# A two-layer decoder step on one core: the first norm's squares and product, the score pairs and the final norm are placed anew

## The chip, the cores and the metric

The kernel runs on one core of one Trainium2 chip. TensorE (PE) multiplies, VectorE (DVE), ScalarE (ACT) and GpSimd (POOL) work on tiles in SBUF, SyncE (SP) mostly issues DMA transfers, as ACT can too. The metric is the device time of one execution in microseconds; three runs of the kernel before gave 601.29 us as median, from 601.08 to 602.26.

## The reference, cut to what matters

One step of a decoder with two layers for 264 tokens: a prompt of 256 and eight samples of one token each, 1024 features wide. All weights are shared.

```
def rmsnorm(x, g):
    y = xf * lax.rsqrt(jnp.mean(xf * xf, axis=-1, keepdims=True) + EPS)
    return (y * g).astype(x.dtype)
...
def moba_gmlp_mixer(...):          # layer 0
    h = rmsnorm(x, norm_g)
    z = h @ w_in                   # q, k, v, bu, bv of 512 each
    q, k = rope_partial(q), rope_partial(k)
    a = moba_attention(q, k_all, v_all, pos)
    bvn = layer_norm(jax.nn.gelu(bv), sgu_gain)
    b_out = spatial_gating(jax.nn.gelu(bu), bvn, sgu_w, sgu_b)
    return x + jnp.concatenate([a, b_out], -1) @ w_out, new_kv, bvn
...
def conv_ffn(...):
    h = rmsnorm(x, norm_g)
    a = jax.nn.gelu(causal_conv(h @ w_gate)) * (h @ w_up)
    return x + a @ w_down, ...
```

Layer 1 has stick-breaking attention and a pooling mixer in place of the two mixers of layer 0; a final rmsnorm gives y. The outputs are y, the new keys and values of both layers, and some small states.

## The kernel before, in words

Activations lie transposed: 128 features on the partitions, the 264 tokens (T) along the free axis, so the 1024 features are eight tiles (KD) of 128 x 264. Every weight matrix is cut into blocks of 128 x 128, and all blocks of the whole step stand in memory in the order in which TensorE uses them: 1472 blocks, one stream. Eight blocks make a tile of the stream. A chunk of one tile (chunks 0 to 5) or two (from chunk 6 on) comes by one DMA (`raw`, line 279). To keep fp32 accuracy each tile is split into a high part wh (an ACT copy, line 299, or line 631 for the first tiles) and a rest wl (a DVE subtraction, line 300 or 632); four buffers each, so a split runs up to three tiles ahead (`LOOK`). Each operand is split alike (xg_h, xg_l; `operand_tile`, line 384). A block is three matmuls: wh by xh, wh by xl, wl by xh. `run` (line 305) walks the order of a phase, asks for splits, issues the three matmuls, calls `evac` when an output tile is complete, and calls hooks that are due at a certain block; `blk(b, f)` (line 863) puts f behind block b of the phase.

The phases are, for each layer: in (160 or 128 blocks), out, ff (gate and up), dn (down). The change touches the first phase, in0, and what comes after the last.

The start: six packed pieces (`xw`) bring the first two tiles of weights and x; ACT, DVE and POOL work in an order that the source fixes with `keep_in_program_order` (lines 634 to 650); everything else is ordered by the planner of the tile framework, which runs its own model of the times. In in0 the first four output tiles, bv, are computed before the first norm's scale is known. The squares of x (ACT, `Norm.add`, line 397) are summed by POOL (lines 408 and 411); the last square stays alone, so the sum over partitions is made by two matmuls with a tile of ones into one PSUM bank (`rstd_of`, line 424; one matmul in fp32 is two rows in the trace). Ln and Exp on ACT (lines 431, 432) turn it into R. This is `norm0` (line 654), a hook behind block 30; it also scales the rope tables by R and then evacuates the bv tiles that were held. From block 32 on q, from 64 on k, from 96 on bu, from 128 on v are computed; their evacuations (lines 687 to 695) use R. `s_qk(t)` (line 707) multiplies q and k of a pair of heads: first a mask matmul (line 710), then the scores S (lines 712, 714); `s_tr` transposes their softmax. `gm_mean` and `gm_var` (lines 814, 817) are the layer norm of the gating branch: the sum over four tiles (bsum, lines 802 to 804), a product with ones (pmu), and the squares. SP issues nearly all DMAs in the order of the source; `page_regs` (line 338) loads page numbers into registers on the same queue, each of them three small instructions.

The end: the last phase evacuates each of its eight output tiles into X (line 598), squares it, lets POOL add the square, and multiplies X by the final gain (line 603). After the last tile come its add, its square, two products with ones (ns_fin), Ln and Exp, five multiplications by R over 1, 2, 2, 2 and 1 feature tiles (line 1109, `YD`), and after each the DMA of its part of y from SP or ACT (line 1110).

Of the kernel before, what the change touches and what calls it, by code (L numbers as in the profile page):

```python
# [18 lines left out]
P = 128  # L19
# [3 lines left out]
NS = 8  # L23
# [12 lines left out]
MMB = 4  # L36
KQ = 5
WARM = 12
YD = ((0, 1), (1, 3), (3, 5), (5, 7), (7, 8))

NEG = -1e30
SCALE = HD ** -0.5
# [108 lines left out]
def _consts():  # L151
# [41 lines left out]
    ("sguw", (P, 512)), ("sgub", (P, 512)), ("poolw", (P, 512)),  # L193
]
_OUTS = [
    ("y", (KD, P, T)), ("k0", (P, 4, T)), ("v0", (P, 4, T)), ("bvn", (P, 4, NS)),
    ("k1", (P, 4, T)), ("v1", (P, 4, T)), ("poolp", (P, 4, NST)), ("pools", (P, 4, NS, 16)),
    ("cv0", (P, NF, 10)), ("cv1", (P, NF, 10)), ("cs0", (P, NF, NS)), ("cs1", (P, NF, NS)),
]
# [3 lines left out]
def tile_decoder_step(ctx: ExitStack, tc: tile.TileContext, a):  # L203
# [30 lines left out]
    def mv(name):  # L234
        return [f4(f"{name}_{x}", dt=F32R) for x in "hl"]
# [37 lines left out]
    def late(dst, src):  # L273
        tc.keep_in_program_order(nc.sync.dma_start(dst, src))
# [14 lines left out]
    pos = [0]  # L289

    def split(t):
        for tt in range(len(splits), min(t + (2 if t == 3 else LOOK), NT - 1) + 1):
            ci = chunk_of[tt]
            for c in range(ci, min(ci + 3, len(_CHUNKS))):
                raw(c)
            o = (tt * 8 - coff[ci]) * P
            src = raws[ci][:, o:o + 8 * P]
            h, l = splits[tt] = wtiles(tt)
            s.activation(h, src, AF.Copy)  # L299
            v.tensor_tensor(l, src, h.bitcast(F32), ALU.subtract)  # L300
        return splits[t]

    spare = (32, 40)
# [34 lines left out]
    def page_regs(n):  # L338
        for i in range(len(regs), len(regs) + n):
            regs.append(nc.sync.value_load(PT[0:1, i:i + 1], min_val=0, max_val=NPHYS - 1))  # L340
# [16 lines left out]
        page_regs(2)  # L357
    late(CS, a["rope"].rearrange("p (c t) -> p c t", c=2))
    raw(5)
    page_regs(4)  # L360
    late(CST, a["cst"])
    raw(6)
    page_regs(4)
    late(VEC, a["vec"])
    page_regs(4)
    GAIN = first[0][0]
    xin = [x[:, i, :] for _, _, x in first for i in range(x.shape[1])]
    tc.keep_in_program_order(s.preload_act_table_set("natural_log_exp_and_others"))
# [21 lines left out]
            tc.keep_in_program_order(j)  # L390

    class Norm:
        def __init__(self, name, two=False):
            self.name, self.two, self.last = name, two, []
            self.acc = None

        def add(self, m, src=None):
            q = sm.tile([P, T], F32, tag="sq", name=f"sq_{self.name}{m}")
            i = s.activation(q, X[:, m, :] if src is None else src, AF.Square)
            if src is not None:  # L400
                tc.keep_in_program_order(i)
            if m == KD - 1 and self.two:
                self.last.append(q)
            elif self.acc is None:
                self.acc = q
            elif m == 1:
                n = sm.tile([P, T], F32, tag="acc", name=f"acc_{self.name}", bufs=2)
                g.tensor_tensor(n, self.acc, q, ALU.add)
                self.acc = n
            else:  # L410
                g.tensor_tensor(self.acc, self.acc, q, ALU.add)

        def finish(self, pin=False):
            return rstd_of([self.acc] + self.last, 1.0 / D, self.name, pin)
# [6 lines left out]
        def finish2(self):  # L421
            return rstd_of(self.hl, 1.0 / D, self.name, w=onesr)

    def rstd_of(parts, scale, name, pin=False, bank=None, w=None):
        p = (bank or at)(f"ns_{name}")
        for i, x in enumerate(parts):
            mm = pe.matmul(p[:, :T], ones if w is None else w, x, start=i == 0, stop=i == len(parts) - 1)
            if pin:
                tc.keep_in_program_order(mm)
        R = sm.tile([P, T], F32, tag="R", name=f"R_{name}", bufs=2)  # L430
        s.activation(R, p[:, :T], AF.Ln, bias=epst, scale=scale)
        last[0] = s.activation(R, R, AF.Exp, scale=-0.5)
        return R

# [114 lines left out]
    def ffn(l, xg, nrm, down_evac, hooks=None):  # L549
# [7 lines left out]

        def norm():
            nonlocal R
            R = nrm.finish2()  # L560
            gelu_set()


# [25 lines left out]
        lnexp()  # L589
        run(orders[f"dn{l}"], lambda m, k: hl(act, k), down_evac, hooks)  # L590

    def residual(gain, name, operand=True):
        xg = [mv(f"xg_{name}{i}") for i in range(2)] if operand else None
        nrm = Norm(name, not operand)

        def evac(m, o):
            m = m[1]
            v.tensor_tensor(X[:, m, :], X[:, m, :], o, ALU.add)
            if operand:
                operand_tile(xg[m // 4], m, X[:, m, :], gain[:, m:m + 1])  # L600
            nrm.add(m)
            if not operand:
                s.activation(X[:, m, :], X[:, m, :], AF.Copy, scale=gain[:, m:m + 1])
        return xg, nrm, evac

    def pick(xg):
        return lambda m, k: hl(xg, k)
# [3 lines left out]


    xg = [mv(f"xg_0{i}") for i in range(2)]
    nrm = Norm("n0", True)
    for tt in range(2):
        splits[tt] = wtiles(tt)

# [19 lines left out]
    for m in range(1, 5):  # L637
        part(m, s)()
        operand_tile(xg[m // 4], m, xin[m], GAIN[:, m:m + 1], pin=True)
        if m != 2:  # L640
            nrm.add((m - 1) // 2 if m < 4 else 2, xin[(m - 1) // 2 if m < 4 else 2])
    whole(2)
    for m in range(5, KD):
        operand_tile(xg[m // 4], m, xin[m], GAIN[:, m:m + 1], pin=True)
    for m in range(3, KD):
        nrm.add(m, xin[m])
        if m == 4:
            whole(3)
        elif m == 6:
            whole(4)  # L650
    rope = f4("rope")
    R0, held = [], []
# [291 lines left out]
    st1 = {}  # L944

    qz1 = sample_z("l1")

    def norm1():
        nonlocal R
        R = nrm1.finish2()  # L950
        sigmoid_set()

    edge = f4("edge", (P, 384))
# [150 lines left out]
    _, nrm, evac = residual(vec("fin"), "fin", operand=False)  # L1104
    ffn(1, xg, norm_f, evac)
    R = nrm.finish()
    for i, (m, e) in enumerate(YD):
        x = X[:, m:e, :]
        v.tensor_tensor(x, x, R.unsqueeze(1).to_broadcast([P, e - m, T]), ALU.mult)  # L1109
        (s if i % 2 else nc.sync).dma_start(a["y"][m:e].rearrange("m p t -> p m t"), x)  # L1110


def _lay(inp):
# [66 lines left out]
```

## Time and profile before

| what | value |
|---|---|
| median of three runs | 601.29 us (601.08 to 602.26) |
| the profiled execution, its own time | 602.49 us |
| its span, first to last instruction | 600.7 us |
| mean granted TensorE clock | 0.995 |
| DVE, ACT, POOL busy in the span | 422.9, 343.3, 107.9 us |
| DMA | 122.42 MB, mean 204 GB/s |

A row of the timeline gives start, duration (both us), engine, line, operation, what it writes and reads with the shape, and how often it is repeated in the row; in square brackets stand the idle time of the engine ahead of it and what ended it. PE is TensorE's matmuls, PEld its weight loads; a "q" behind an engine is its queue. In a row of stretches come the stretch, its length, the busy time and number of instructions for each engine shown, the granted clock, the busy share of the DMA engines, and GB/s. Matmuls overlap in the pipeline, so that a PE row's duration is longer than its slot.

### The profile page before, as it was taken

The numbers are of one execution on the slowest core, as the hardware profiler recorded it, in microseconds if no ns is written. First come the engines' busy times: TensorE is split into PE (matmuls) and PEld (weight loads), VectorE is DVE, ScalarE is ACT, GpSimd is POOL, SyncE is SP. The second block draws the span as 40 slices with busy tenths as digits, with TensorE's granted clock in tenths as the row PEclk, the third lists the DMA queues.
The fourth block names the chain that finished last, engine by engine and source line by source line (L and its number), as shares of the span: only waits on it lengthen the run. The fifth ranks groups of instructions, "written<-read, shape, count | busy, mean of one in ns | idle before, by whom it ended". The sixth has DMA issues, their size and how long they took to land.

```text
span 600.7 us, 12394 instructions
## 1 busy us (share of the span) xinstructions
PE 588.6 (98%) x4900; PEld 569.6 (95%) x4900; DVE 422.9 (70%) x733; ACT 343.3 (57%) x600; POOL 107.9 (18%) x103
## 2 busy tenths in 40 slices
PE   8999999999999999999999999999999999999994
PEld 6988879999999999999999879999999999999994
DVE  7899565977778777665559676687777777864432
ACT  7657754675655656644454466657656565564441
POOL 4100002303222232210120000031232323211110
PEclk9999999999999999999999999999999999999998
DMA  8998835454555545795467763554545454555402
GB/s 319 337 399 323 316 121 202 152 201 152 200 170 182 186 165 202 264 378 214 155 247 256 261 203 113 174 204 148 201 154 206 147 205 159 193 187 202 181 1 74
DMA packets 28092, 122.42 MB, mean 204 GB/s; under 512 B 3330, under 2 KB 5250, under 8 KB 16642
## 3 DMA queue, kind: packets, MB, share of 16 engines
q1 hardware_dynamic: 27200, 120.42, 56.1%
q10 hardware_dynamic: 834, 1.20, 0.6%
q8 instruction: 39, 0.64, 0.4%
q14 instruction: 19, 0.16, 0.1%
HBM read 117.65 MB, written 3.96 MB: 202 GB/s over the span
## 4 chain that ended last, share of the span: by engine, by line
PE 92%; DVE 3%; DMA 2%; SPq 1%; issue 1%; ACT 0%; ACTq 0%; DVEq 0%
PE mm L215 85%; DMA raw<-in_w 1%; PE pv_l L215 1%; PE sc L215 1%; DVE wl L300 1%; PE pav L215 1%; PE pt L218 1%; DMA PT<-in_pt 1%; PE S L215 1%; SPq L340 1%; PE Z L215 1%; PE pf L215 0%; DVE X L1109 0%; PE pm L215 0%; DVE rz_q L687 0%
## 5 line engine op out<-in xcount | busy, mean ns | idle before, releaser
L300 DVE TENSOR_TENSOR wl<-raw,wh 128x1024 fp32r<-128x1024 f32 x179 | 218.9, 1224 | 78.1 <-ACT wh L299 77.9
L299 ACT ACTIVATE wh<-raw 128x1024 fp32r<-128x1024 f32 x179 | 188.6, 1055 | 92.7 <-PE mm L215 84.1
L215 PE MATMUL mm<-xg_f_h,wh 128*128 128x264 f32 x704 | 200.1, 284 | 0.0
L215 PE MATMUL mm<-xg_f_l,wh 128*128 128x264 f32 x704 | 199.9, 284 | 0.0
L215 PE MATMUL mm<-xg_f_h,wl 128*128 128x264 f32 x704 | 198.6, 282 | 0.0
L215 PEld LDWEIGHTS mm<-xg_f_l,wh 128*128 128x128 f32 x704 | 132.3, 188 | 0.0
L215 PEld LDWEIGHTS mm<-xg_f_h,wh 128*128 128x128 f32 x704 | 132.2, 188 | 0.0
L215 PEld LDWEIGHTS mm<-xg_f_h,wl 128*128 128x128 f32 x704 | 132.2, 188 | 0.0
L582 POOL TENSOR_TENSOR wk<-wk 128x264 f32<-128x264 f32 x44 | 66.5, 1513 | 193.9 <-DVE wk L581 159.3
L215 PE MATMUL mm<-a_h,wh 128*128 128x264 f32 x352 | 100.1, 284 | 0.0
L215 PE MATMUL mm<-a_l,wh 128*128 128x264 f32 x352 | 99.9, 284 | 0.0
L215 PE MATMUL mm<-a_h,wl 128*128 128x264 f32 x352 | 99.4, 282 | 0.0
L215 PEld LDWEIGHTS mm<-a_l,wh 128*128 128x128 f32 x352 | 66.1, 188 | 0.0
L215 PEld LDWEIGHTS mm<-a_h,wh 128*128 128x128 f32 x352 | 66.1, 188 | 0.0
L215 PEld LDWEIGHTS mm<-a_h,wl 128*128 128x128 f32 x352 | 66.1, 188 | 0.0
L442 ACT ACTIVATE a_h<-wk 128x264 fp32r<-128x264 f32 x44 | 18.7, 424 | 73.3 <-POOL wk L582 73.3
L215 PE MATMUL mm<-xg_h,wh 128*128 128x264 f32 x160 | 47.5, 297 | 1.1 <-ACT xg_h L386 1.1
L443 DVE TENSOR_TENSOR a_l<-wk,a_h 128x264 fp32r<-128x264 f32 x44 | 19.2, 437 | 41.5 <-ACT a_h L442 41.5
L215 PE MATMUL mm<-xg_h,wl 128*128 128x264 f32 x160 | 45.7, 285 | 0.7 <-DVE wl L632 0.6
L215 PE MATMUL mm<-xg_l,wh 128*128 128x264 f32 x160 | 45.6, 285 | 0.1
L215 PE MATMUL mm<-xg_n_h,wh 128*128 128x264 f32 x128 | 38.4, 300 | 0.0
L215 PE MATMUL mm<-xg_n_l,wh 128*128 128x264 f32 x128 | 36.3, 283 | 0.0
(245 smaller groups left out, 897.3 us busy)
## 6 DMA issues: line engine op xcount, KB each, us to landing
raw<-in_w SPq DMA_DIRECT2D x89, 1024.0 KB, 4.8
K<-in_kt SPq DMA_DIRECT2D x32, 256.0 KB, 6.7
V<-in_vp SPq DMA_DIRECT2D x32, 256.0 KB, 5.2
raw<-in_w SPq DMA_DIRECT2D x4, 512.0 KB, 5.7
X<-in_x SPq DMA_DIRECT2D x4, 264.0 KB, 6.4
xw<-in_xw SPq DMA_DIRECT2D x2, 388.0 KB, 5.5
out_k<-k SPq DMA_DIRECT2D x1, 528.0 KB
out_v<-v SPq DMA_DIRECT2D x1, 528.0 KB, 5.0
```

The lines of the kernel that those rows point to most:

```text
L215: return self.keep(nc.tensor.matmul(*x, **k))
L218: return self.keep(nc.tensor.transpose(*x, **k))
L299: s.activation(h, src, AF.Copy)
L300: v.tensor_tensor(l, src, h.bitcast(F32), ALU.subtract)
L340: regs.append(nc.sync.value_load(PT[0:1, i:i + 1], min_val=0, max_val=NPHYS - 1))
L442: s.activation(h, src, AF.Copy)
L443: v.tensor_tensor(l, src, h.bitcast(F32), ALU.subtract)
L582: g.tensor_tensor(A, A, C, ALU.mult)
```

## The change

Four things are changed.

1. The first norm. The squares of x stand later in the fixed order: four after tile 3's split, one and a wide one over three feature tiles after tile 4's. They go into two tiles of four squares; POOL sums the first four (one add of two tiles wide, one of one), DVE the other four in the same way, and then both sums. The product with ones is now one matmul, behind block 34. Tile 5's wl is ordered behind the sum, and a wh of a tile below 8 behind the Exp, if the norm has been issued by then.
2. SP's queue at the start: raw6 directly behind raw5; eight register loads in one go behind CST; the small vectors (VEC) behind block 64.
3. Score pairs from blocks 82 and 95 to 86 and 97, `gm_var` from 108 to 113.
4. The end by halves of the tokens (132 columns): add and square of the last tile, the product of its square, Ln and Exp, the multiplications and the transfers. y is laid out as two halves of (P, KD, 132). The last tile's gain is applied in its multiplication by R.

```diff
     def split(t):
...
-            s.activation(h, src, AF.Copy)
-            v.tensor_tensor(l, src, h.bitcast(F32), ALU.subtract)
+            i = s.activation(h, src, AF.Copy)
+            if R0 and tt < 8:
+                behind(i, last[0])
+            i = v.tensor_tensor(l, src, h.bitcast(F32), ALU.subtract)
+            if tt == 5:
+                behind(i, summed)
...
     raw(5)
+    raw(6)
     page_regs(4)
     late(CST, a["cst"])
-    raw(6)
-    page_regs(4)
-    late(VEC, a["vec"])
-    page_regs(4)
+    page_regs(8)
...
+    def final():
+
+        nrm = Norm("fin")
+        gain = vec("fin")
+        halves_ = [slice(0, TH), slice(TH, T)]
+        sq = sm.tile([P, T], F32, tag="R", name="sq_last", bufs=2)
+        keep = tc.keep_in_program_order
+
+        def evac(m, o):
+            m = m[1]
+            if m < KD - 1:
+                v.tensor_tensor(X[:, m, :], X[:, m, :], o, ALU.add)
+                nrm.add(m)
+                s.activation(X[:, m, :], X[:, m, :], AF.Copy, scale=gain[:, m:m + 1])
+                return
+            for c in halves_:
+                keep(v.tensor_tensor(X[:, m, c], X[:, m, c], o[:, c], ALU.add))
+                keep(s.activation(sq[:, c], X[:, m, c], AF.Square))
+
+        def rest():
+            p = at("ns_fin")
+            R = sm.tile([P, T], F32, tag="R", name="R_fin", bufs=2)
+            keep(pe.matmul(p[:, :T], ones, nrm.acc, start=True, stop=False, skip_group_check=True))
+            for c in halves_:
+                keep(pe.matmul(p[:, c], ones, sq[:, c], start=False, stop=True, skip_group_check=True))
+
+            def rstd(c):
+                keep(s.activation(R[:, c], p[:, c], AF.Ln, bias=epst, scale=1.0 / D))
+                keep(s.activation(R[:, c], R[:, c], AF.Exp, scale=-0.5))
+
+            for c in halves_:
+                rstd(c)
+            for i, c in enumerate(halves_):
+                Y = f4(f"y{i}", (P, KD, TH))
+                cuts = ((0, 4), (4, 8)) if i == 0 else ((0, 4), (4, 6), (6, 8))
+                for n, (m, e) in enumerate(cuts):
+                    w = min(e, KD - 1)
+                    keep(v.tensor_tensor(Y[:, m:w, :], X[:, m:w, c], R[:, c].unsqueeze(1).to_broadcast([P, w - m, TH]), ALU.mult))
+                    if e == KD:
+                        keep(v.scalar_tensor_tensor(Y[:, w, :], X[:, w, c], gain[:, w:w + 1], R[:, c], ALU.mult, ALU.mult))
+                    (s if n % 2 else nc.sync).dma_start(a["y"][i][:, m:e, :], Y[:, m:e, :])
+        return evac, rest
...
     for m in range(1, 5):
         part(m, s)()
         operand_tile(xg[m // 4], m, xin[m], GAIN[:, m:m + 1], pin=True)
-        if m != 2:
-            nrm.add((m - 1) // 2 if m < 4 else 2, xin[(m - 1) // 2 if m < 4 else 2])
     whole(2)
     for m in range(5, KD):
         operand_tile(xg[m // 4], m, xin[m], GAIN[:, m:m + 1], pin=True)
-    for m in range(3, KD):
-        nrm.add(m, xin[m])
-        if m == 4:
-            whole(3)
-        elif m == 6:
-            whole(4)
+    whole(3)
+    keep = tc.keep_in_program_order
+    sq0 = [f4(f"sq0_{i}") for i in range(2)]
+
+    def sum0(e, q):
+
+        keep(e.tensor_tensor(q[:, 0:2, :], q[:, 0:2, :], q[:, 2:4, :], ALU.add))
+        keep(e.tensor_tensor(q[:, 0, :], q[:, 0, :], q[:, 1, :], ALU.add))
+
+    for m in range(4):
+        keep(s.activation(sq0[0][:, m, :], xin[m], AF.Square))
+    sum0(g, sq0[0])
+    whole(4)
+    keep(s.activation(sq0[1][:, 0, :], xin[4], AF.Square))
+    keep(s.activation(sq0[1][:, 1:4, :], first[5][2], AF.Square))
+    sum0(v, sq0[1])
+    summed = keep(v.tensor_tensor(sq0[1][:, 0, :], sq0[0][:, 0, :], sq0[1][:, 0, :], ALU.add))
...
     def norm0():
-        R = nrm.finish(pin=True)
+        R = rstd_of([sq0[1][:, 0, :]], 1.0 / D, "n0", True)
...
-    blk(30, norm0)
+    blk(34, norm0)
...
+    blk(64, late, VEC, a["vec"])
...
-    for t, b in enumerate((82, 95, 108, 121)):
+    for t, b in enumerate((86, 97, 108, 121)):
...
-    blk(108, gm_var)
+    blk(113, gm_var)
...
-    R = nrm.finish()
-    for i, (m, e) in enumerate(YD):
-        x = X[:, m:e, :]
-        v.tensor_tensor(x, x, R.unsqueeze(1).to_broadcast([P, e - m, T]), ALU.mult)
-        (s if i % 2 else nc.sync).dma_start(a["y"][m:e].rearrange("m p t -> p m t"), x)
+    rest()
```

More of the change, by code (lines that the diff above doesn't have):

```diff
@@ L38 @@
 WARM = 12
-YD = ((0, 1), (1, 3), (3, 5), (5, 7), (7, 8))
+TH = T // 2
 NEG = -1e30
@@ L289, in tile_decoder_step @@
     pos = [0]
+    R0 = []
     def split(t):
@@ L392, in tile_decoder_step, with __init__, add @@
     class Norm:
[L393 to L397, printed above, removed]
+        def __init__(self, name):
+            self.name, self.acc = name, None
+        def add(self, m):
             q = sm.tile([P, T], F32, tag="sq", name=f"sq_{self.name}{m}")
[L399 to L404, printed above, removed]
+            s.activation(q, X[:, m, :], AF.Square)
+            if self.acc is None:
                 self.acc = q
@@ L559, in norm @@
             nonlocal R
-            R = nrm.finish2()
+            R = nrm.finish()
             gelu_set()
@@ L590, in ffn, with residual @@
         run(orders[f"dn{l}"], lambda m, k: hl(act, k), down_evac, hooks)
-    def residual(gain, name, operand=True):
-        xg = [mv(f"xg_{name}{i}") for i in range(2)] if operand else None
-        nrm = Norm(name, not operand)
+    def residual(gain, name):
+        xg = [mv(f"xg_{name}{i}") for i in range(2)]
+        nrm = Norm(name)
         def evac(m, o):
@@ L644, in tile_decoder_step @@
         operand_tile(xg[m // 4], m, xin[m], GAIN[:, m:m + 1], pin=True)
-    for m in range(3, KD):
-        nrm.add(m, xin[m])
-        if m == 4:
-            whole(3)
-        elif m == 6:
-            whole(4)
+    whole(3)
[12 more added lines that the diff above has]
+    summed = keep(v.tensor_tensor(sq0[1][:, 0, :], sq0[0][:, 0, :], sq0[1][:, 0, :], ALU.add))
     rope = f4("rope")
-    R0, held = [], []
+    held = []
     def norm0():
-        R = nrm.finish(pin=True)
+        R = rstd_of([sq0[1][:, 0, :]], 1.0 / D, "n0", True)
         R0.append(R)
@@ L946, in tile_decoder_step @@
     qz1 = sample_z("l1")
+    R = None
     def norm1():
         nonlocal R
-        R = nrm1.finish2()
+        R = nrm1.finish()
         sigmoid_set()
```

17 lines of the change are left out of this document (6 added, 11 removed).

## The prediction, made before the change was run

> **What bounds the kernel now.** I read the page's first lines, then PE's waits, then PE's starts one by one in the two places where it does not stream, then the other engines there.
>
> ```profile
> span 600.7 us, 12394 instructions
> PE 588.6 (98%) x4900; PEld 569.6 (95%) x4900; DVE 422.9 (70%) x733; ACT 343.3 (57%) x600; POOL 107.9 (18%) x103
> ```
> ```profile
> 121.97 191.11 PE mm L215 x1578
> ```
>
> TensorE bounds it. The second row, from the chain of work that ended last, is one unbroken stretch of the stream: 191.11 / 1578 = 0.121 us a matmul, 0.363 us a block of three. From about 40 us to 591 us PE waits for nobody, so a change can only win before 40 us, where the pipeline is being filled, or after the last matmul. PE's list of waits agrees (who waited for whom, us in total, times, longest):
>
> ```profile
> PE S L215 <- DVE k L693: 1.0, 1, 1.0
> PE ns_fin L215 <- ACT sq_fin L399: 0.6, 1, 0.6
> PE mm L215 <- DVE wl L632: 0.6, 1, 0.6
> ```
>
> The list hides short waits, since a matmul is drawn until its modelled end. Counting matmuls in equal stretches shows them (stretch, length, PE busy, matmuls):
>
> ```profile
> 11.80:17.80 6.00, 5.41 (x41) 1.00 0.89 296
> 22.00:28.00 6.00, 6.00 (x52) 1.00 0.98 373
> ```
>
> 41 against 52: eleven slots of 0.121, **1.33 us**, are lost between 12 and 18 us, at full granted clock. The cause stands on DVE:
>
> ```profile
> 12.20 2.30 DVE L387 SCALAR_TENSOR_TENSOR xg_l<-xw,xw,xg_h 128x264 fp32r<-128x264 f32 x3
> 14.43 3.47 DVE L632 TENSOR_TENSOR wl<-raw,wh 128x1024 fp32r<-128x1024 f32 x2
> 17.82 1.21 DVE L300 TENSOR_TENSOR wl<-raw,wh 128x1024 fp32r<-128x1024 f32 x1
> 22.01 1.23 DVE L300 TENSOR_TENSOR wl<-raw,wh 128x1024 fp32r<-128x1024 f32 x1 [2.98 <-ACT wh L299]
> ```
> ```profile
> 12.46 4.35 POOL L411 TENSOR_TENSOR acc_n<-acc_n,sq_n 128x264 f32<-128x264 f32 x4 [1.61 <-ACT sq_n L399]
> ```
> ```profile
> 585.02 0.75 POOL L411 TENSOR_TENSOR acc_fin<-acc_fin,sq_fin 128x264 f32<-128x264 f32 x1 [5.12 <-ACT sq_fin L399]
> ```
>
> A wl pass takes 1.21 us alone and 3.47 / 2 = 1.74 beside POOL's adds; the adds take 4.35 / 4 = 1.09 there and 0.75 alone. PE starves on these DVE passes.
>
> **The first norm.** Its product is two matmul pairs on PE at block 30, its R comes on ACT, and the chain runs on to the first score pair:
>
> ```profile
> 18.32 0.61 PE L215 MATMUL ns_n<-acc_n,ones 128*128 128x264 f32 x2
> 18.77 0.39 PE L215 MATMUL ns_n<-sq_n,ones 128*128 128x264 f32 x1
> ```
> ```profile
> 16.00 0.41 ACT L399 ACTIVATE sq_n<-xw 128x264 f32<-128x264 f32 x1
> 20.91 1.06 ACT L299 ACTIVATE wh<-raw 128x1024 fp32r<-128x1024 f32 x1 [4.50 <-DMA raw<-in_w]
> 21.88 0.47 ACT L431 ACTIVATE R_n<-ns_n,epst 128x264 f32<-128x264 f32 x1
> 22.37 0.43 ACT L432 ACTIVATE R_n<-R_n 128x264 f32<-128x264 f32 x1
> ```
> ```profile
> 9.70 0.43 SPq L274
> ...
> 12.82 7.99 DMA raw<-in_w
> ```
> ```profile
> 38.11 0.39 PE L215 MATMUL S<-maskb,identb 128*128 128x256 bf16 x2
> 39.49 0.38 PE L215 MATMUL S<-k,q 64*128 64x128 f32 x2 [0.99 <-DVE k L693]
> ```
> ```profile
> 39.01 0.43 DVE L693 TENSOR_TENSOR k<-k,rz_k 128x264 f32<-128x264 f32 x1
> ```
>
> The product is over by about 19.3, yet Ln waits until 21.88 because tile 6's wh stands before it on ACT and waits for raw6 (issued at 12.82, landed at 12.82 + 7.99 = 20.81). R is there at 22.80. From R to the end of k at 39.44 are 16.64 us, which the chain of work spends on DVE alone (rope, the four held bv tiles, q, k, and wl passes between them), and PE waits 0.99 for that k.
>
> **The change, part by part.**
>
> *Squares later and wide.* Removed: the squares between the first splits, and POOL's six adds beside DVE's passes. Both DVE rows above then cost what they cost alone, the two wl passes 2.3 us in place of 3.47, and PE's 1.33 us go: **−1.33** (bounds: 0 if what takes their place crowds DVE alike, −1.33 if nothing does). Added: ACT squares of 4 × 264 elements, one of 264 and one of 792. By rows of 264 and of 1056 elements ACT costs 0.86 ns an element and DVE 1.15:
>
> ```profile
> 57.05 1.09 ACT L824 ACTIVATE sq<-bv 128x1056 f32<-128x1056 f32 x1
> ```
> ```profile
> 54.91 1.34 DVE L822 TENSOR_TENSOR bv<-bv,mu 128x1056 f32<-128x1056 f32 x1
> ```
>
> so the 792 take 0.41 + 0.45 = 0.86, no more than three single ones. ACT had done all squares and tile 5's wh by 16.41; without that wh (about 0.95, now behind) the last square ends at about 15.5. Counted back from there (0.86, 0.33, a wh of 0.97) the fourth square ends near 13.5, so POOL adds 528 and then 264 elements from about 13.6: at most 1.5 + 0.75, till 15.9. DVE adds 528, 264 and 264: 0.73 + 0.43 + 0.43, less the overlap of neighbours, 1.4, from about 16: the sum stands at 17.3 to 17.5. PE asks for it at block 34: 18.32 − 1.33 + 4 × 0.363 = 18.44. Cover: 1 us; when it is gone, every 0.1 us of lateness is 0.1 us of PE. Behind the waiting product stands the whole stream.
>
> *One product for two.* The second began 0.45 after the first: **−0.45** (bounds −0.3 to −0.45).
>
> *raw6 ahead of four register loads and CST.* It is issued straight behind raw5, at 10.2 for 12.82, so I let it land 2.6 earlier, 18.2 (later than 20.81 nothing puts it; at the earliest some 17.3). Splits of tiles 6 and 7 are still asked for at block 32, before the product at 34, when R0 is empty: the new order "behind the Exp" is never drawn for them, and the planner places Ln. With both wh ahead of it (0.97 each, 20.91 to 21.88) Ln starts at 20.1 and R is there at 21.0; with Ln first, product over at 19.0, at 19.95. I take 20.8. VEC's transfer moves behind block 64 on SP's queue, its first reader is at block 130: nothing. The eight register loads in one go hold the same queue as long as two times four.
>
> *Score pairs 82→86, 95→97; gm_var 108→113.* Block 86's pair is asked for at 38.11 − 1.33 − 0.45 + 1.45 = 37.78, its k side 0.3 later, 38.1. k is ready at R + 16.64 = 37.4, sooner by 1.14 for every wl pass that DVE does in the 2.98 us in which it stood idle before 22.01. So the wait goes: **−1.0**. Next late is gm_var: its input is
>
> ```profile
> 52.37 0.43 DVE L804 TENSOR_TENSOR bsum<-bsum,bv 128x264 f32<-128x264 f32 x1
> ```
> ```profile
> 53.12 0.64 PE pmu L215 x2
> ```
>
> 0.3 us ahead of PE; PE comes 2.78 earlier and, by five blocks, 1.82 later, DVE 1.1 to 2 earlier: nothing, with a cover of a few tenths.
>
> *Halves of tokens at the end.* Before, all in one line:
>
> ```profile
> 591.62 0.43 DVE L598 TENSOR_TENSOR X<-X,mm 128x264 f32<-128x264 f32 x1 [7.56 <-PE mm L215]
> ```
> ```profile
> 592.62 0.73 PE ns_fin L215 x2
> ```
> ```profile
> 593.88 0.42 ACT L432 ACTIVATE R_fin<-R_fin 128x264 f32<-128x264 f32 x1
> ```
> ```profile
> 594.33 2.63 DVE L1109 TENSOR_TENSOR X<-X,R_fin 128x264 f32<-128x264 f32 x5 [2.29 <-ACT R_fin L432]
> ```
> ```profile
> 594.79 2.58 SPq L1110 DMA_DIRECT2D out_y<-X  x3
> ```
> ```profile
> 597.00:599.00 2.00, 0.00 (x0) 0.00 (x0) 0.00 (x0) 0.00 (x0) 0.00 (x0) 0.50 1.03 355
> 599.00:600.70 1.70, 0.00 (x0) 0.00 (x0) 0.00 (x0) 0.00 (x0) 0.00 (x0) 0.50 0.04 12
> ```
>
> By the slopes, 132 elements save 0.15 on DVE and 0.11 on ACT; the add, the square, Ln and Exp of the first half are 0.48 shorter together and its product by about 0.2: R's first half at 593.6 for 594.30. The products with R then run 528, 396, 132, 528, 264, 132, 132 elements; two instructions more at some 0.08 each: 2.8 us for 2.63, ending at 596.4 for 596.96. The output is 1.08 MB, at the 355 GB/s of the last stretch 3.05 us, and the DMA engines are full from 597 until just after 599: the end is the start of the flow plus 3.05. The first issue comes at 594.3 for 594.79 and carries 270 KB for 135, so the flow no longer runs thin at first; it may end 0.8 sooner. By the last multiplication alone it is 0.55; when Ln of the first half must wait for the second half's product in the same bank, 0.2 less. Value **−0.7**, bounds 0 and −0.9. The Trainium skill, "PSUM — Partial Sum Buffer", section "PSUM bank collisions raise a hardware error", has a rule that speaks against these halves: guard PSUM by bank and quadrant, not by address. By it the sum would be −0.5 here; no row of this profile shows which the kernel's waits follow.
>
> **Sum.** −1.33 − 0.45 − 1.0 − 0.7 = −3.5 us: span 600.7 → 597.2, the profiled execution 602.49 → 599.0. The profiled execution is 1.2 above the median of the runs, 601.29, and about 1.8 of it lies outside the span; the change touches only the span, so the median goes to **597.8**.
>
> **Rivals.**
>
> *The sum comes late.* POOL's 528-element add falls beside wl4. If each engine blocks the other for whole instructions, wl4 (from 14.6) waits for POOL's first add until 15.1, POOL's second for wl4 until 16.3, DVE's adds for POOL's until 17.1, and the sum is there at 18.4, just in time; one more such turn, 1.2 us, and PE waits 1.2: **599.0**. For it: the rows where a pass took 1.74 for 1.21. Against: 1 us of cover. Chance 0.10. The Trainium skill, "SBUF — State Buffer", section "Who interferes with whom", states such a lock, held for the whole instruction by whichever started first, for a DVE operation with two SBUF inputs against a reading GpSimd one; the rows agree in size, 0.53 being less than one add of 0.75.
>
> *k stays where it is.* If R comes no sooner (raw6 lands at 20.8 all the same, since the queue is full), k is ready at 39.44 and the pair, asked for at 38.1, waits 1.3 in place of 0.99: the start wins 1.5, **599.1**. For: the chain lies on DVE from R to k without a gap that could be closed. Against: the 2.98 idle ahead of it and the earlier issue. Chance 0.15.
>
> *The tail gives nothing*, as transfers in pieces of 132 columns flow no faster and two issues more do not help: **598.5**. Chance 0.12.
>
> *Slower: Ln behind tile 8's wh.* The order "behind the Exp" binds no tile here, so it doesn't do what it says, and the planner may put one more split before Ln. That split is this one:
>
> ```profile
> 24.70 1.06 ACT L299 ACTIVATE wh<-raw 128x1024 fp32r<-128x1024 f32 x1 [0.35 <-DVE bv L695]
> ```
>
> Ln would start at 25.7, R be there at 26.6, 3.8 later than now, k at 43.3 for a PE that is there at 38.1 or, held at block 48 for bv's banks, at 42. Block 86 with its pair then ends at 44.2, against 39.49 + 0.9 + 1.45 = 41.8 now: +2.4, less 0.7 of the tail: **603.0**. It decides from R at about 25 us. Chance 0.12.
>
> **How the numbers follow.** Forecast 0.51, with its own range 597.2 to 598.5; late sum 0.10, late k 0.15, tail 0.12, slower 0.12. Low end: all bounds at their best, −4.0, and 0.3 of scatter: 597.0. High end: late k together with a dead tail, and some scatter: 600.2; outside stay the slower case and a few hundredths. About 0.2%, 1.2 us, is what a measurement of this kernel can tell from no change. Late sum and late k together win only some 1.0: 0.08 for "same", taken from these two. Faster 0.80, slower 0.12.
>
> **What would show it.** Right: about 52 matmuls between 11.8 and 17.8 us; wl passes of 1.21 from 11 us on; one ns_n pair after a wait of nothing at about 18.4; Ln before 20.5; no wait of S for k; ns_fin in three parts and the first out_y issue within 2.8 us of the last X add's start (3.17 now). Wrong: a wait of PE on ns_n for DVE's sum; Ln behind a wh that waits for a transfer; S waiting for k again; pmu waiting for bsum; DMA flow ending at the same distance, 7.4 us, behind that add.

## The result and the profile after

The changed kernel takes 600.37 us (median of 13 runs, 598.9 to 600.79) against 601.68 us for the kernel before, run beside it (13 runs, 601.08 to 603.38): a ratio of **0.9972, 95% interval 0.9963 to 0.9981**. The medians lie 1.3 us apart, the means 1.7, and the ratio, which weighs all runs, says 1.7. The forecast was 597.8, 3.5 us faster, with a range up to 600.2: the sign was right, the size about half, and the time lies just outside the range.

The profiled execution of the changed kernel took 600.75 us, with a span of 598.8. Its profile, first lines:

```profile
span 598.8 us, 12383 instructions
PE 589.5 (98%) x4900; PEld 571.7 (95%) x4900; DVE 423.4 (71%) x739; ACT 343.1 (57%) x600; POOL 104.5 (17%) x99
```

PE's list of waits (who waited for whom, us in total, times, longest):

```profile
PE warm L215 <- DVE warm L373: 1.2, 1, 1.2
PE mm L215 <- ACT xg_h L389: 0.7, 1, 0.7
PE ns_fin L215 <- ACT sq_last L616: 0.3, 1, 0.3
```

The waits for `wl` and for the keys are gone, as forecast. What the forecast put in their place is there too: one product for the norm where there were two, Ln behind tiles 6 and 7 (ACT), k at 37.40 where 37.4 was forecast (DVE), and a first score pair whose products follow its masks without a wait:

```profile
20.00 0.61 PE L215 MATMUL ns_n<-sq,ones 128*128 128x264 f32 x2
```
```profile
18.34 2.07 ACT L300 ACTIVATE wh<-raw 128x1024 fp32r<-128x1024 f32 x2 [1.44 <-DMA raw<-in_w]
20.64 0.48 ACT L427 ACTIVATE R_n<-ns_n,epst 128x264 f32<-128x264 f32 x1 [0.23 <-PE ns_n L215]
```
```profile
36.97 0.43 DVE L737 TENSOR_TENSOR k<-k,rz_k 128x264 f32<-128x264 f32 x1
```
```profile
39.35 0.39 PE L215 MATMUL S<-maskb,identb 128*128 128x256 bf16 x2
39.67 0.93 PE L215 MATMUL S<-k,q 64*128 64x128 f32 x8
```

But look at the starts. PE comes to the norm's product at 20.00 where the forecast had 18.44, and to the score pair at 39.67 where it had 38.1. Ln starts at 20.64, right behind the product, where the forecast asked for one before 20.5. PE itself is 1.6 us late, with nobody to wait for. The matmuls counted in equal stretches show where (stretch, length, PE busy and matmuls, granted clock, share of the DMA engines, GB/s); first the changed kernel, then before:

```profile
6.00:10.30 4.30, 4.30 (x22) 1.00 1.04 415
11.80:17.80 6.00, 6.00 (x51) 1.00 0.96 327
```
```profile
6.00:10.30 4.30, 4.24 (x34) 1.00 1.03 411
```

From 11.8 on the stream is whole (51, where the forecast asked for about 52 and before had 41). From 6.0 to 10.3 it is not: 22 matmuls against 34, PE busy all the time, and the granted clock reads 1.00 in both. One by one, changed kernel and then before:

```profile
8.09 0.42 PE L215 MATMUL mm<-xg_l,wh 128*128 128x264 f32 x1
8.31 0.42 PE L215 MATMUL mm<-xg_h,wl 128*128 128x264 f32 x1
```
```profile
6.29 0.28 PE L215 MATMUL mm<-xg_l,wh 128*128 128x264 f32 x1
6.41 0.28 PE L215 MATMUL mm<-xg_h,wl 128*128 128x264 f32 x1
```

The starts lie 0.22 us apart in the one and 0.12 in the other. The changed kernel ran the first products of its stream, up to 10.3 us, at **half rate**, 20 of them 0.10 us too slow, 2.0 us together; the execution of before that the forecast was read from did not. (PE is 1.6 late and not 2.0 because its first product started at 4.64 us here, at 5.08 there.) The clock column doesn't show it; the count of matmuls does.

The tail gave about what the forecast said. From the last add to the end of the span:

```profile
590.34 0.49 DVE L615 TENSOR_TENSOR X<-X,mm 128x132 f32<-128x132 f32 x2 [7.56 <-PE mm L215]
591.03 0.72 PE L215 MATMUL ns_fin<-sq_last,ones 128*128 128x132 f32 x4 [0.28 <-ACT sq_last L616]
591.78 0.37 ACT L626 ACTIVATE R_fin<-ns_fin,epst 128x132 f32<-128x132 f32 x1 [0.60 <-PE ns_fin L215]
...
593.26 2.52 SPq L639 DMA_DIRECT2D out_y<-y  x3
```
```profile
595.00:597.00 2.00, 0.00 (x0) 0.00 (x0) 0.42 (x2) 0.00 (x0) 0.00 (x0) 0.50 1.02 365
597.00:599.00 2.00, 0.00 (x0) 0.00 (x0) 0.00 (x0) 0.00 (x0) 0.00 (x0) 0.50 0.08 27
```

598.8 − 590.34 is 8.46 us, where before had 600.7 − 591.62 = 9.08: **−0.62**. The first issue comes 2.92 behind the add (3.17 before; under 2.8 was forecast), and the DMA engines are done just after 597, two microseconds sooner on the clock.

So every part of the change can be seen at work, and 2.0 us were paid back before 10.3 us. The question for the experiments: is the half rate an accident of this one execution, something that the change brings about, or something that both kernels have, and that the kernel before hides?

### The profile page after: what moved, and what is told of

It is laid out like the page before. It is cut to its first block, busy times and chain, and to the rows that moved or that the text cites. A ratio compares the mean times of both kernels' runs of the same rounds, so it can differ in the third digit from the quotient of the medians.

```text
span 598.8 us, 12383 instructions
## 1 busy us (share of the span) xinstructions
PE 589.5 (98%) x4900; PEld 571.7 (95%) x4900; DVE 423.4 (71%) x739; ACT 343.1 (57%) x600; POOL 104.5 (17%) x99
## 4 chain that ended last, share of the span: by engine, by line
PE 98%; DMA 1%; DVE 0%; ACT 0%; DVEq 0%; issue 0%
PE mm L215 90%; PE pv_l L215 1%; PE sc L215 1%; PE pav L215 1%; PE pt L218 1%; PE S L215 1%; PE Z L215 1%; DMA xw<-in_xw 1%; PE pf L215 0%; DVE y L636 0%; PE pm L215 0%; PE vtp_v L218 0%; PE po_l L218 0%; PE vtp_sgu L218 0%; PE ns_fin L215 0%; PE ns_n L215 0%
## 5 line engine op out<-in xcount | busy, mean ns | idle before, releaser
L215 PE MATMUL mm<-xg_h,wh 128*128 128x264 f32 x160 | 48.8, 305 | 0.7 <-ACT xg_h L389 0.7
```

Of the source, the lines that this page charges most:

```text
L215: return self.keep(nc.tensor.matmul(*x, **k))
```

## The experiments

Theory A: the half rate belongs to the start of both kernels in most executions. Before hides it, because its first score pair waits for the keys anyway; the changed kernel waits for nothing, and so pays for every slow product. Theory B: it was an accident of one profile and explains no times. Theory C: something in the change costs 1 to 2 us elsewhere. All medians, with their runs, and the ratio to the kernel before on the same chip (its medians there 602.02 to 602.16):

| run | median us (lowest to highest, runs) | ratio to before, 95% | matmuls 6.0 to 10.3 us |
|---|---|---|---|
| after_again | 599.89 (599.03 to 600.50, 5) | 0.9958 (0.9945 to 0.9971) | 23 |
| after_third | 600.23 (599.74 to 600.69, 7) | 0.9968 (0.9957 to 0.9980) | 24 |
| after_w16 | 599.19 (598.94 to 600.78, 6) | 0.9956 (0.9943 to 0.9968) | 35 |
| after_fill | 599.27 (599.06 to 599.59, 5) | 0.9955 (0.9942 to 0.9969) | 36 |
| after_fill_b | 599.15 (599.09 to 599.76, 5) | 0.9951 (0.9937 to 0.9964) | 33 |
| after_w2 | 600.71 (599.84 to 601.16, 7) | 0.9974 (0.9963 to 0.9985) | 21 |
| before_w16 | 601.83 (601.09 to 603.97, 12) | 1.0000 (0.9990 to 1.0009) | 21 |
| before_fill | 602.40 (601.22 to 603.73, 11) | 1.0005 (0.9995 to 1.0015) | 37 |
| before_w2 | 602.12 (601.71 to 602.83, 11) | 1.0003 (0.9994 to 1.0012) | 29 |
| tail_only | 601.41 (600.67 to 602.49, 12) | 0.9991 (0.9983 to 1.0000) | 23 |
| before_raw6 | 601.42 (601.12 to 601.80, 11) | 0.9986 (0.9977 to 0.9995) | 23 |
| before_fill_raw6 | 601.27 (600.95 to 601.34, 11) | 0.9985 (0.9976 to 0.9994) | 37 |
| fill_raw6_back | 600.39 (599.79 to 601.46, 9) | 0.9975 (0.9965 to 0.9984) | 35 |
| fill_pairs_back | 600.13 (599.41 to 601.36, 9) | 0.9971 (0.9961 to 0.9981) | 22 |
| fill_banks | 599.41 (598.80 to 600.93, 6) | 0.9960 (0.9946 to 0.9973) | 33 |
| fill_banks_b | 598.88 (598.74 to 600.89, 5) | 0.9956 (0.9942 to 0.9969) | 35 |

The last column is from one profile of each: 21 to 24 is half rate throughout, 33 to 37 is full rate.

**The same kernels again, with more warm-up, and the tail alone.** The edit of the two runs with 16:

```diff
-WARM = 12
+WARM = 16
```

after_again is the changed kernel unaltered:

> The changed kernel once more, for another profiled execution and more times. Theory A (the first matmuls of the stream run at half rate for some microseconds, and the changed kernel, whose start no longer waits for anything else, pays for each of them; before hid them behind its waits): time 600.0 to 600.7; the number of matmuls at 0.22 us spacing after the first three may be anything from 0 to 26, and the span falls by 0.10 us for each one fewer than 20. Theory B (the half rate was an accident of the one profiled execution and has no part in the times): no half-rate matmuls, and the time still 600.4. Theory C (a part of the change costs 1 to 2 us elsewhere): time 600.4 and a place after 12 us at which PE waits or falls behind.

> The changed kernel with 16 warm-up matmuls for 12, so that TensorE works without a pause until its first product at about 4.8 us. Theory A: the half rate ends by 8.3 us at the latest and sooner on the average, so that 5 to 20 of the 20 half-rate matmuls become full-rate ones: 598.4 to 599.8. Theories B and C: 600.2 to 600.7, since nothing on the path changes.

> The kernel before with 16 warm-up matmuls for 12. Theory A: the start there is set by weight tiles and by the keys, so nothing moves: 601.2 to 602.0. Theory B: the same. If the half rate cost the kernel before as much as the changed one, 600.0 to 600.8.

tail_only is the kernel before with only these lines (and `final` with its output layout) from the change:

```diff
-    _, nrm, evac = residual(vec("fin"), "fin", operand=False)
+    evac, rest = final()
     ffn(1, xg, norm_f, evac)
-    R = nrm.finish()
-    for i, (m, e) in enumerate(YD):
...
+    rest()
```

> The kernel before with only the part behind the stream's last tile by halves of tokens; the start is that of before. All theories that take the traces of the two tails at their word: 0.65 us less than before, 601.0. If the tail's gain is lost in the kernel's end: 601.6. If the tail carried all of the gain: 600.2.

Measured: 599.89 (0.1 under the band of Theory A), 599.19, 601.83 and 601.41. The half rate is back in after_again, and it is also in the two kernels that have the *old* start, before_w16 and tail_only, here in that order:

```profile
6.00:10.30 4.30, 4.30 (x21) 1.00 1.03 414
11.80:17.80 6.00, 6.00 (x52) 1.00 0.91 299
```
```profile
6.00:10.30 4.30, 4.30 (x23) 1.00 1.03 419
11.80:17.80 6.00, 6.00 (x52) 1.00 0.94 334
```

So the change doesn't bring it about. And the second rows say more: in these executions the old start has no hole between 11.8 and 17.8 us, 52 matmuls against the 41 of the forecast. A PE that is 1.5 us behind no longer overtakes its low halves; the 1.33 us that the forecast subtracted were not there to be gained. before_w16's time didn't move (ratio 1.0000), which fits A and B; after_w16 fell 0.7 under after_again, inside A's band, but the two intervals overlap. tail_only's time lies between the two expected values 601.0 and 601.6, but before took 602.10 beside it; it is 0.5 us under before (interval 0 to 1.0), about what the trace of the changed kernel's end says, and doesn't carry the whole gain.

**The rate forced both ways.** Fillers behind the first three products, which are spaced wider than a product takes anyway, and 16 warm-ups:

```diff
+FILL = [256, 128, 128]
...
+                if i == 0:
+                    f = FILL[j]
+                    pe.matmul(pw[:, :f], warm[:, :P], warm[:, :f], start=True, stop=True)
```

and, the other way, `WARM = 2`. Each in both kernels.

> The changed kernel with TensorE kept at work without a gap from 1.2 us: 16 warm-up matmuls for 12, and one more warm-up matmul behind each of the first three products (256, 128 and 128 columns), where the stream waits anyway. Theory A, as the first runs have left it (three of four of the kernels with 12 warm-ups ran their first 17 to 20 products at 0.22 us; the kernel before loses nothing by that, since its weight tiles and keys come no sooner, the changed kernel loses 0.10 us for each): most executions are at full rate by 8 us, and the time is 598.3 to 599.3. Theory C (the rest of the forecast gain is lost in a part of the change): 600.0 to 600.6, as without the fillers.

> The kernel before with the same warm-ups and fillers. Theory A: what TensorE gains in the first 10 us it waits for afterwards, 1.3 us for low halves of weight tiles and up to 1.0 us for the keys at the first score pair: 601.2 to 602.2, no gain. If the kernel before gains from the full rate too (its waits were an accident of one execution): 600.0 to 601.0.

> The changed kernel with 2 warm-up matmuls for 12: the half rate then holds in every execution until at least 8 us. Theory A: no execution under 599.7, 600.3 to 601.0. Theory C: 600.4.

> The kernel before with 2 warm-up matmuls for 12. Theory A: 601.4 to 602.3, so that with the half rate in every execution the change is worth 1.0 to 1.5 us (one norm product for two, 0.45, and the tail, 0.65), against 2.6 to 3.4 us between the two kernels with fillers. If the half rate doesn't matter, both differences are the 1.7 us of the change itself.

Measured: 599.27 and 602.40 with fillers, 600.71 and 602.12 with two warm-ups. With fillers the change is worth 3.1 us, with two warm-ups 1.4. Both differences are as Theory A had them (2.6 to 3.4, and 1.0 to 1.5), and the kernel before stays where it was, 602.1 to 602.4, the latter 0.2 above its band. Its profiles say why. With fillers (full rate), then with two warm-ups (half rate until 8 us):

```profile
6.00:10.30 4.30, 4.30 (x37) 1.00 1.04 415
11.80:17.80 6.00, 5.43 (x41) 1.00 0.91 293
```
```profile
39.05 0.93 PE L216 MATMUL S<-k,q 64*128 64x128 f32 x8 [0.82 <-DVE k L696]
```
```profile
39.27 0.93 PE L215 MATMUL S<-k,q 64*128 64x128 f32 x8 [1.07 <-DVE k L693]
```

The pair starts at 39.05, at 39.27, at 39.49 in the execution of the forecast, whatever PE did in the first 10 us: in these three it starts when k is there. (In before_w16 and tail_only, where PE was later and tile 6 sooner, it starts at 38.83 and 38.36 and waits for nobody.) In the changed kernel it starts when PE is there, with fillers at 38.00, without at 39.67:

```profile
6.00:10.30 4.30, 4.30 (x36) 1.00 1.04 420
11.80:17.80 6.00, 6.00 (x52) 1.00 0.87 318
```
```profile
37.68 0.39 PE L216 MATMUL S<-maskb,identb 128*128 128x256 bf16 x2
38.00 0.93 PE L216 MATMUL S<-k,q 64*128 64x128 f32 x8
```

38.00 is the 38.1 of the forecast, and the span of after_fill, 597.1, is its 597.2; from before_fill's 600.3 that is 3.2 us. after_w2's fastest time, 599.84, is above the floor of 599.7 that a half rate in every execution sets.

**Which part gives the keys sooner.** The load of weight tile 6 alone, put into the kernel before (with fillers, and later without), and taken back out of the changed one (with fillers; the reverse of this edit):

```diff
     raw(5)
+    raw(6)
     page_regs(4)
     late(CST, a["cst"])
-    raw(6)
```

> The kernel before with fillers (602.4), with the load of weight tile 6 moved ahead of the constants, as the change has it, and nothing else of the change. Theory A: Ln no longer stands behind a tile that lands at 20.5, R and the keys come some 1.5 us sooner, and the wait of 0.8 to 1.0 at the first score pair goes, while the waits for low halves of weight tiles stay: 601.2 to 601.8. Rival (the waits come from the squares and the norm, not from the load): 602.1 to 602.7.

> The changed kernel with fillers (599.27), with the load of weight tile 6 put back behind the constants and four register loads, where the kernel before has it. Theory A: its ACT copy stands ahead of Ln on the queue and starts at about 20.5 us again instead of 18.7, Ln, R and the keys come 0.9 to 1.3 us later (keys at 38.2 to 38.6 against 37.3), and TensorE, which asks for the first score pair at 38.0, waits 0.2 to 0.6: 599.4 to 599.9. Rival: the earlier load is worth nothing, since the pair is asked late enough: 599.1 to 599.4.

Measured: 601.27, 1.1 us under before_fill, as A expected. ACT's rows, first of before_fill, then with the load ahead:

```profile
20.46 1.06 ACT L300 ACTIVATE wh<-raw 128x1024 fp32r<-128x1024 f32 x1 [4.06 <-DMA raw<-in_w]
21.42 0.46 ACT L434 ACTIVATE R_n<-ns_n,epst 128x264 f32<-128x264 f32 x1
```
```profile
18.08 1.06 ACT L300 ACTIVATE wh<-raw 128x1024 fp32r<-128x1024 f32 x1 [1.14 <-DMA raw<-in_w]
19.24 0.48 ACT L434 ACTIVATE R_n<-ns_n,epst 128x264 f32<-128x264 f32 x1
```

Ln comes 2.2 us sooner, and the wait at the score pair is off PE's list, while the wait for low halves stays:

```profile
PE ns_fin L216 <- ACT sq_fin L402: 0.6, 1, 0.6
PE mm L216 <- DVE wl L635: 0.6, 1, 0.6
```

The spread goes too: 601.22 to 603.73 before, 600.95 to 601.34 after. Behind the constants tile 6's copy started at 19.5, 19.9, 20.5, 20.7 and 20.9 us in the five profiles of the kernel before and its versions; ahead of them at 18.0 and 18.1. That the scatter of the kernel before was this one transfer is likely and not shown. Nor does the transfer land more steadily ahead of the constants: in the ten profiles of the changed kernel and its versions that have it there, tile 6's copy starts anywhere from 17.7 to 19.4. It lands sooner, and so is less often what Ln waits for: in before_raw6 Ln waits for the norm's product.

Taken out of the changed kernel, the load cost 1.1 us (600.39), nearly twice the most that was expected, and not by the wait that was expected. The profiled execution, 601.46, was the slowest of the nine:

```profile
21.08 2.01 ACT L301 ACTIVATE wh<-raw 128x1024 fp32r<-128x1024 f32 x2 [4.73 <-PE mm L216]
23.00 0.46 ACT L430 ACTIVATE R_n<-ns_n,epst 128x264 f32<-128x264 f32 x1
```
```profile
26.06 0.36 PE L216 MATMUL mm<-xg_h,wh 128*128 128x264 f32 x1 [2.07 <-DVE bv L742]
```

(The first row names PE, since a matmul ended just then. By the trace's semaphore times tile 6 had landed 0.1 us before the copy started, and it is the tile that the copy waited for.) With the product at block 34 both tile 6 and tile 7 stand ahead of Ln, R comes at 23.9, and PE stops for 2.07 us at 24, long before the score pair: the accumulators of bv wait for R, and the stream has no bank left. That is the stall which the forecast named in its slower case ("held at block 48 for bv's banks"); it needs R at 23.9, not at 25, and the earlier load is what keeps it away.

**The score pairs back.** In the changed kernel with fillers:

```diff
-    for t, b in enumerate((86, 97, 108, 121)):
+    for t, b in enumerate((82, 95, 108, 121)):
...
-    blk(113, gm_var)
+    blk(108, gm_var)
```

> The changed kernel with fillers, with the score pairs at blocks 82 and 95 and the gmlp variance at 108, where the kernel before has them. Theory A: the first pair is asked 4 blocks, 12 slots of 0.121 us or 1.46 us, sooner, at 36.5, and the keys come at 37.3 still: a wait of 0.7 to 0.8, and 599.8 to 600.1. Rival: the place of the pairs is worth nothing: 599.1 to 599.4.

Measured: 600.13, just above the band, in three heaps (three times 599.41 to 599.61, three 600.03 to 600.37, three 601.11 to 601.36). This is **inconclusive**: the profiled execution was at half rate in spite of the fillers, and in it the pair came at 38.49 with k there at 37.67, no wait at all:

```profile
6.00:10.30 4.30, 4.30 (x22) 1.00 1.03 416
```
```profile
37.24 0.43 DVE L740 TENSOR_TENSOR k<-k,rz_k 128x264 f32<-128x264 f32 x1
```

Whether the pairs' place or the rate made the times higher, these runs don't tell.

**The last norm in two PSUM tiles.** In the changed kernel Ln of the first half starts at 591.78, when both halves' products are over. The edit gives each half its own tile, for the product of the sum too:

```diff
-            p = at("ns_fin")
+            ps = [at(f"ns_fin{i}") for i in range(2)]
...
+            for p, c in zip(ps, halves_):
+                keep(pe.matmul(p[:, :TH], ones, sq[:, c], start=False, stop=True, skip_group_check=True))
```

> The changed kernel with fillers, with the two halves of the last norm's products in two PSUM tiles, so that Ln of the first half needs nothing of the second. In the changed kernel Ln of the first half starts 0.04 us behind the end of the second half's product. If it is that product it waits for: Ln starts 0.2 us sooner and the span behind the last add is 8.2 us for 8.45, 599.0 to 599.2. If it is the first half's own product, or the tile doesn't matter: 8.4 to 8.5 us as before, 599.2 to 599.4.

Measured: 599.41, above both bands by its median and too scattered to tell from after_fill's 599.27, but the trace is plain:

```profile
589.01 0.49 DVE L618 TENSOR_TENSOR X<-X,mm 128x132 f32<-128x132 f32 x2 [7.56 <-PE mm L216]
...
590.24 0.37 ACT L630 ACTIVATE R_fin<-ns_fin,epst 128x132 f32<-128x132 f32 x1 [0.38 <-PE ns_fin L216]
```

Ln starts 1.23 behind the add, for 1.44 in the changed kernel and in after_fill, and the span ends 597.2 − 589.01 = 8.2 behind it for 8.46. With one tile for both, the half that was ready waited 0.2 us for its neighbour. The halves of one tile share a bank, so these runs don't tell whether the kernel's waits go by the tile or by the bank. The Trainium skill, "PSUM — Partial Sum Buffer", section "PSUM bank collisions raise a hardware error", asks for a guard by the bank and not by the address; the waits in this pair of traces are as such a guard makes them.

**Side by side.** The changed kernel with and without fillers and with two tiles, timed side by side, and the load alone without fillers:

> The changed kernel a third time, beside the version with fillers in one call. If the half-rate start is where the missing part of the forecast went: 0.6 to 1.4 us above after_fill_b, most times between 599.8 and 600.8 and a few near 599.0. If it isn't: the two within 0.3 us of each other.

> The changed kernel with fillers again: 599.0 to 599.6, with single times up to 601 where an execution starts at half rate all the same.

> Fillers and the last norm's halves in two PSUM tiles, again: 0.2 us under after_fill_b by the trace of its end, 598.8 to 599.4.

> The kernel before with nothing changed but the place of the load of weight tile 6, ahead of the constants. With the half rate TensorE comes to the first score pair at 38.4 to 38.8 and the keys are there at 37.4: 600.9 to 601.4, a spread under 0.8 us for 2.3 before. If the load is worth nothing without the rest: 601.7 to 602.2.

Measured: 600.23, 599.15, 598.88 and 601.42. The fillers are worth 1.08 us to the changed kernel, and nothing to the one before (before_fill 1.0005). Of 25 times of the unaltered changed kernel only 4 are at or under 599.76; all ten of after_fill and after_fill_b are (the intervals of after_third and after_fill_b still overlap a little). before_raw6 is 0.02 above its band, and its times span 0.7 us for 2.6 of the kernel before beside it. fill_banks_b has the lowest median of all; its interval (0.9942 to 0.9969) doesn't part it from after_fill_b, and one time in each of the two runs with two tiles is 600.9. By the medians either one is faster than both kernels of this case.

Theory A stands. B fell with the half rate in five of the six profiles that have 12 warm-ups and no fillers, and with the 1.08 us; C with after_fill, where nothing of the change was altered and the span came out as forecast. Why one execution starts at half rate and another does not stays open.

## Why the prediction was right in sign and wrong in size

- **The list of waits before: right for one execution.** The forecast took its waits from the one profile that it had, an execution of 602.49 us, 1.2 above the median of the runs then shown. That execution had full rate from 6.2 us, as no other of the six profiles with 12 warm-ups and no fillers, *and* the latest tile 6 of five (20.9). Of these five profiles, with the old start and the load in its old place, two have no wait at the score pair, and the same two have no hole at 12 us. From the median of all executions the sum subtracted 2.33 us of waits (1.33 and 1.0) that this one execution had.
- **"−1.33, the low halves": the step that failed first.** It says that PE's slots between 11.8 and 17.8 us go "at full granted clock". The mechanism is real, at full rate: before_fill has 41 matmuls there and after_fill 52. The size is right there too: before_fill_raw6 comes to the product behind block 30 at 18.15, after_fill to the one behind block 34 at 18.33, and 4 × 0.363 − 0.18 is 1.27 us. At half rate, which is the usual start, before has 52 there too, and the term is about 0: the product behind block 30 comes at 18.24, 18.30 and 18.72 in tail_only, before_raw6 and before_w16, the one behind block 34 at 19.62, 19.75 and 20.00 in the three profiles of the changed kernel, some 1.4 later, which is the four blocks (1.45). What the forecast put at nothing is PE's own rate at the start.
- **"So the wait goes: −1.0": a price of one execution.** The wait was 1.0, 0.8 and 1.1 us in three profiles and nothing in two. Undone alone, by the earlier load, it is worth 0.14% (0.05 to 0.23), 0.8 us. The cause, raw6 ahead of Ln, was right. That k came at 37.4 was in part luck: R came at 21.58 for 20.8, and from R to k it took 15.8 us for 16.64 (the forecast had left room for that, but not reckoned with it). In the changed kernel R is late since PE came to the norm's product 1.6 late; in after_fill, where the product starts at 18.33, R comes at 21.58 as well, since Ln stands behind two copies that begin when raw6 has landed, at 18.74 where the forecast let it land at 18.2:

```profile
18.74 2.01 ACT L301 ACTIVATE wh<-raw 128x1024 fp32r<-128x1024 f32 x2 [1.80 <-DMA raw<-in_w]
20.66 0.46 ACT L430 ACTIVATE R_n<-ns_n,epst 128x264 f32<-128x264 f32 x1
```

- **"−0.45, one product for two": right**, one pair of matmuls in place of two in every profile of the new start. From the product to the masks of the first score pair, 52 blocks in both kernels, are 39.35 − 20.00 = 19.35 us in the changed kernel and 38.11 − 18.32 = 19.79 before.
- **"−0.7, the halves": right in size, by two misses that cancel in part.** It is 0.62 by the trace, 0.5 (0 to 1.0) alone by the times. The forecast took no wait of the first half for the second; that wait is there and costs 0.2, and the rest of the tail gave 0.1 to 0.2 more than was reckoned.
- **The sum of squares in time: right, with 0.2 us of cover for 1.** The forecast had the sum at 17.3 to 17.5. In after_fill it ends at 17.69 + 0.43 = 18.12 and PE asks for it at 18.33. The rival "the sum comes late" is what is seen, turn by turn, only without its last turn:

```profile
13.52 1.34 POOL L687 TENSOR_TENSOR sq<-sq 128x528 f32<-128x528 f32 x1 [11.08 <-ACT sq L691]
14.94 1.62 POOL L688 TENSOR_TENSOR sq<-sq 128x264 f32<-128x264 f32 x1
```
```profile
14.42 1.52 DVE L670 TENSOR_TENSOR wl<-raw,wh 128x1024 fp32r<-128x1024 f32 x1 [0.80 <-ACT wh L669]
15.86 1.26 DVE L687 TENSOR_TENSOR sq<-sq 128x528 f32<-128x528 f32 x1
```

  The last wl pass took 1.52 for 1.21 beside POOL's first add, POOL's second add 1.62 for 0.75 beside that pass, and DVE's first add 1.26 for the 0.73 that was reckoned beside POOL's second. So the passes are not all 1.21 long from 11 us on, as the forecast asked.
- **gm_var: right**, pmu at 53.68 without a wait.
- **The rivals.** The late sum came in its mechanism and cost PE nothing; the others did not come. What did come, PE itself as the bound of the start, was on no list, though one row of the very profile that was read held a sign of it:

```profile
1.20 2.74 PE L215 MATMUL warm<-warm 128*128 128x256 bf16 x12 [1.20 <-DVE warm L370]
```

  Twelve matmuls of 256 columns in 2.74 us are 0.23 us each, where the stream takes 0.121 for 264: TensorE starts at half rate, and the warm-up had ended before that changed.

The books at full rate, by the spans of three profiles: before_fill 600.3; with the load ahead 599.5, 0.8 less, which is its wait of 0.82 for the keys; after_fill 597.1, 2.4 less, which is 1.27 + 0.44 + 0.62 within 0.1. That is 3.2, and 3.1 by the times, for 3.5. At half rate: before_raw6 599.6, the changed kernel 598.4 to 598.8, 0.8 to 1.2 less, for 0.44 + 0.62 and nothing for the low halves. The load is worth 0.8 there by the times, an average over executions that wait for the keys and others that don't, so that 1.75 to 1.85 stand against 1.7 measured. These are sums of parts taken from few profiles; they fit, and no run checks the sum by itself.

## What to carry to other kernels

Removing a wait moves the bound to whatever is next late, and where that is an engine's own rate over a stretch that the old kernel waited through, the old profile has no row for it; ask of each stretch how fast the engine could go there if nothing held it, and count instructions in equal stretches instead of trusting a clock column. Price a wait from several executions when the time scatters by more than the wait: a wait that comes from one transfer's landing is a distribution, and after moving that transfer the kernel before scattered by 0.4 us for 2.5, while its median fell by 1.1 (both with fillers). When a kernel begins with warm-up work, check in its trace that the work has the effect it is there for.

## What was not expected of the hardware

The half rate at the start ends at very different times: by 6.5 us in nine of 18 profiles, seven of them with fillers, at 8.0 in before_w2, between 9.4 and 10.6 in seven others, at 11.2 in after_w2. Keeping PE at work makes full rate likely, not certain: seven of the eight profiles with fillers have it by 6.5 us, one of the six with 12 warm-ups and none. In fill_pairs_back PE worked from 1.2 us on with one recorded pause,

```profile
4.95 0.59 PE L216 MATMUL mm<-xg_h,wh 128*128 128x264 f32 x1 [0.16 <-ACT xg_h L392]
```

and its products started about 0.22 us apart until 10.1 us, 8.9 us after its first warm-up. The Trainium skill, "TensorE: Matmul & The Clock Gate", Part 1 ("The HAM clock gate"), describes half rate by default, released by about 3.4 us of sustained work, at a point that differs from run to run. The half rate and the variation agree with these traces (0.22 against 0.12 us; 6.2 to 11.2 us); the 3.4 us don't agree with this one.
